# Beginning the first three products of a hybrid SSD / RG-LRU block on half of the tokens

## The chip, the cores and the metric

The kernel runs on one core of one Trainium2 chip. The metric is the device time of one execution in microseconds (us), the median of several executions. A core has a matmul engine (TensorE, PE in the profile, with PEld for its weight loads), a vector engine (VectorE, DVE), a scalar engine (ScalarE, ACT), GpSimd (POOL) and SyncE (SP), which here issues the transfers between main memory and the core's SBUF. Each engine takes its instructions in order, and engines wait for one another on semaphores. PE writes only to PSUM, which has eight banks of 128 partitions by 512 floats.

## The reference

One residual block over x [512 tokens, 1024 channels], float32:

```
h = rmsnorm(x, mix_pre_norm)
u = h @ w_in                                  # [ssd z | ssd x,B,C | ssd dt | lru gate | lru x | merge gates]
y_a = ssd_mixer(u_z, u_xbc, u_dt, ...)        # conv4, chunked state-space scan, gated norm
y_b = rglru_mixer(u_ly, u_lx, ...)            # conv4, gated linear recurrence
merged = g0 * (y_a @ w_proj_ssm) + g1 * (y_b @ w_proj_lru)
x = x + rmsnorm(merged @ w_out, mix_post_norm)
h = rmsnorm(x, ffn_pre_norm)
up = causal_dwconv(h @ w_ffn_up)
x = x + rmsnorm((gelu(up_gate) * up_value) @ w_ffn_down, ffn_post_norm)
```

Here only the first two lines matter: the norm of x along its 1024 channels, and the first three column groups of `h @ w_in`: 128 columns of B (called slab 0), the 16 dt columns padded to a slab (slab 1), and 128 more columns of B (slab 2).

## The kernel before

**Weights.** All weights come as 149 slabs of [128, 1024] floats, in the order of use, loaded one by one on SP's queue into three `raw` buffers. Each slab is split into a high part (`whi`, a cast on ACT) and a low part (`wlo`, a subtraction on DVE), each with three buffers; the dt slab gets no `wlo`, only 16 columns of its `whi` are overwritten with a difference. `prefetch(n)` splits slabs until n of them lie ahead of use, and `low_parts` issues the subtractions that are due.

**Products.** `product(hT)` takes one slab and multiplies it with the activations of all 512 tokens, which are held channel-major in two halves `hT[0]` (high) and `hT[1]` (low), eight tiles of 128 channels each (k = 0 to 7). For each k it issues three matmuls of 128x512 (whi times high, whi times low, wlo times high), 24 for a slab. The dt product issues two for each k, 16 in all.

**The start.** x comes as four token tiles `xts[t]` of [128 tokens, 1024 channels]. For each tile ACT sums the squares (`sumsq`) and takes a root, DVE makes two factors of it by four small instructions (`inv_rms`) and scales the tile (`scale`), and PE turns its eight 128x128 blocks (transposes by a matmul with `ident`) into eight PSUM tiles `tps[k]`, one for each k with all 512 tokens. Ahead of that PE does 24 transposes of `ident` (`WARM`), which use nothing and whose output nobody reads. When all four tiles are turned, the eight `tps[k]` are split into `hT`: `split_scaled` multiplies by the channel's norm weight on ACT (the high part), then takes the difference on DVE (the low part). The splits of slabs 0 and 1 stand among these. Then the products begin.

**What sets the order.** The class `InOrder` keeps ACT's and PE's instructions in the order in which the program writes them, and DVE's until `V.on = False`; after that a scheduler orders DVE. Two engines that read the same PSUM bank wait for each other in the order written. PSUM has eight tiles (`ps`), handed out in turn; a new one waits until the readers of the old one in its bank are done. After each product, `conv` reads its PSUM tile with one ACT and three DVE instructions; `dt_product` copies its result on DVE, and two slabs later `dt_tokens` turns that copy on PE.

The same halving exists before, later in the kernel: around the second norm (`h2_pair`, `early`) the first four products of `w_ffn_up` are begun on tokens 0 to 255, with 128x256 matmuls.

Of the kernel before, what the change touches and what calls it, by code (L numbers as in the profile page):

```python
# [25 lines left out]

# columns of the per-channel parameter array
C_SCW, C_SCB = 0, 48
# [5 lines left out]
N_PC = 356  # L34
# columns of the row parameter array
R_POST, R_POST2, R_HEAD = 0, D, 2 * D
# [3 lines left out]
class InOrder:  # L40
    """An engine whose instructions keep the order in which they are written here."""

# [11 lines left out]
def block_kernel(ctx: ExitStack, tc, x, slabs, wgate, pc, rows, out):  # L54
# [37 lines left out]

# [1 line left out]
    xts = []  # L94
    for t in range(TT):
        xt = quad()
        nc.sync.dma_start(out=xt, in_=x[t * P:(t + 1) * P, :])
        xts.append(xt)
    ident = const.tile([P, P], F32, name="ident")
    make_identity(nc, ident)  # L100
    pcs = const.tile([P, N_PC], F32, name="pcs")
    nc.sync.dma_start(out=pcs, in_=pc)
    hrow = const.tile([P, 48], F32, name="hrow")
    nc.sync.dma_start(out=hrow, in_=rows[0:1, R_HEAD:R_HEAD + 48].partition_broadcast(P))

# [1 line left out]
    pending, steps = [], []  # L107
# [5 lines left out]
    def step(cost, fn, *args):  # L113
        """A step for the vector engine, of that many microseconds."""
        steps.append((cost, fn, args))

    def next_slab():
        """What follows needs the tensor engine to have gone on, or another engine's result."""
        steps.append(None)
# [19 lines left out]

# [1 line left out]
    n_slabs = slabs.shape[0]  # L141
    stream = {"load": 0, "split": 0, "use": 0}
    raws, splits, places, late = {}, {}, {}, []
    AHEAD, EARLY, WARM = 2, 4, 24

# [53 lines left out]
    def split_scaled(hi, lo, src, w):  # L199
        """Split of src * w, w one value per partition."""  # L200
        A.mul(hi, src, w)
        V.scalar_tensor_tensor(out=lo, in0=src, scalar=w, in1=hi.bitcast(F32),
                               op0=ALU.mult, op1=ALU.subtract)
# [7 lines left out]
    def product(acts):  # L211
        """One 128-column slab against [1024, 512] activations: [128 columns, 512 tokens]."""
        w = slab()
        acc = ps()
        accumulate(acc, w, acts)
        return acc

    def conv(acc, w0, bias, taps):
        """Causal depthwise convolution along the tokens."""
        t = tmp()  # L220
        A.activation(t, acc, AF.Identity, bias=pcs[:, bias:bias + 1],
                     scale=pcs[:, w0 + taps - 1:w0 + taps])
# [24 lines left out]

    def inv_rms(parts, width, e):
        """(sum of parts / width + e) ** -0.5, as two factors; one part may be [128, n]."""
        n = parts[0].shape[1]  # L250
# [4 lines left out]
        for s in parts[:-1]:  # L255
# [3 lines left out]
        r = t("root")  # L259
        A.activation(r, parts[-1], AF.Sqrt, scale=1.0 / width, bias=e)  # L260
        v = t("var")
        V.tensor_scalar(out=v, in0=parts[-1], scalar1=1.0 / width, scalar2=e,
                        op0=ALU.mult, op1=ALU.add)
# [12 lines left out]

# [1 line left out]
    use_sqrt()  # L278
    hT = big16("H", F32R), big16("H", F32R)
    junk = work.tile([P, D], F32, tag="M", name="squares", bufs=1)  # L280
    tps = [ps() for _ in range(KT)]
    for k in range(WARM):
        PE.transpose(tps[k % KT][:, 0:P], ident, ident)
    for t in range(TT):
        scale(xts[t], xts[t], inv_rms([sumsq(xts[t], junk=junk)], D, EPS1))
        for k in range(KT):
            transpose(tps[k][:, t * P:(t + 1) * P], xts[t][:, k * P:(k + 1) * P])
    prefetch(1)
    low_parts()
    for k in range(KT):  # L290
        split_scaled(hT[0][:, k, :], hT[1][:, k, :], tps[k], pcs[:, C_PRE + k:C_PRE + k + 1])
        if k == 3:
            prefetch(2)
            low_parts()
    V.on = False

# [1 line left out]
    def causal(value, name):  # L298
        m = const.tile([P, P], F32, name=name)      # value where column >= row
        G.memset(m, value)  # L300
        G.affine_select(out=m, in_=m, compare_op=ALU.is_ge, fill=0.0, base=0,
                        pattern=[[1, P]], channel_multiplier=-1)
        return m
# [4 lines left out]
    G.memset(ones, 1.0)  # L308
    halfb = const.tile([P, 32], F32, name="halfb")  # halves of br, bi, gate_b
    V.tensor_scalar_mul(halfb, pcs[:, C_BR:C_BR + 32], 0.5)  # L310
    nsp4 = const.tile([P, 8], F32, name="nsp4")     # -4 softplus(-lambda)
    nega = const.tile([P, HEADS], F32, name="nega")

    def softplus(u, e):
        """max(u, 0) + log1p(e) with e = exp(-|u|), the logarithm by its atanh series."""
        n = u.shape[1]
# [15 lines left out]

# [1 line left out]
    def ssd_input(j, dst=None):  # L334
# [17 lines left out]
    def dt_product():  # L352
        w = slab()[0]
        acc = ps()
        for k in range(KT):
            c = slice(k * P, (k + 1) * P)
            mm(acc, w[:, c], hT[0][:, k, :], k == 0, False)
            mm(acc, w[:, c], hT[1][:, k, :], False, k == KT - 1)
        raw = tmp()
        V.tensor_copy(raw[:32, :], acc[:32, :])  # L360
        after(2, lambda: dt_tokens(raw))
# [69 lines left out]
    for g in range(2):  # L431
        ssd_input(10 + g, Cc[:, g, :])
        tick()
# [1 line left out]
    xs = big.tile([P, TT, D], F32, tag="C", name="xs", bufs=2)  # L435
# [129 lines left out]

# [1 line left out]
    for j in range(2):  # L567
# [16 lines left out]

# [1 line left out]
    for c in range(2):  # L586
# [80 lines left out]

# [1 line left out]
    m1 = []  # L669
# [23 lines left out]

# [1 line left out]
    def row_tile(r0):  # L695
# [121 lines left out]

# [1 line left out]
    early = []  # L819
# [51 lines left out]
def _layout(x, mix_pre_norm, mix_post_norm, w_in, ssm_conv_w, ssm_conv_b, ssm_dt_bias, ssm_a_log,  # L871
# [70 lines left out]
```

## Time and profile before

| what | value |
|---|---|
| runs | 889.61, 887.66, 887.65 us; median 887.66 |
| the profiled execution | span 885.8 us from first to last instruction; its own time is not listed apart from the three runs |
| what lies around the span, by the median | 887.66 - 885.8 = 1.86 us |
| busy PE / PEld / DVE / ACT / POOL | 872.5 / 724.0 / 519.9 / 392.8 / 1.7 us |
| TensorE clock granted, mean | 0.999 |
| DMA | 91.6 MB, mean 103 GB/s |

The span is what the trace shows of one execution; the time of a run holds some more around it. Busy time of PE counts matmuls from their start to their modelled end. An engine's rows are its instructions in order of time; the note in square brackets is how long it sat idle before the instruction and what ended that.

### The profile page before, as it was taken

Reading aid. Unit: us, or ns where it says so; the run is one execution under the profiler, and the core shown is the slowest. Engines: PE = TensorE matmul, PEld = TensorE weight load, DVE = VectorE, ACT = ScalarE, POOL = GpSimd, SP = SyncE. Lnnn points to the kernel's source line nnn. Section 1 sums busy time; section 2 is a strip of 40 time slices with the busy share of each in tenths; the row PEclk is TensorE's granted clock in tenths of the full one; section 3 lists DMA queues with packets and bytes.
Section 4 is the critical chain, followed back from the end, with each engine's and each line's share of the span. In section 5 each row is a group of like instructions: output and inputs, shape, how many; then the busy total and the mean of one; then the engine's idle time right before and its main releaser. Section 6 shows DMA issues by size and latency. Waiting matters only on the chain.

```text
span 885.8 us, 10176 instructions
## 1 busy us (share of the span) xinstructions
PE 872.5 (98%) x4050; PEld 724.0 (82%) x4050; DVE 519.9 (59%) x732; ACT 392.8 (44%) x602; POOL 1.7 (0%) x14
## 2 busy tenths in 40 slices
PE   7999999999999999999999999999999999999996
PEld 6888887888878888888888988888888888888885
DVE  6777657987874554344467566666666666223225
ACT  6454535579584334222355444444444444213222
POOL 0000000000000000000000000000000000000000
PEclk9999999999999999999999999999999999999999
DMA  6332232222325332222370022222222222322212
GB/s 224 102 137 95 95 118 84 92 87 72 142 96 182 128 119 72 96 95 95 102 252 27 25 94 96 95 95 96 95 95 95 95 95 95 117 98 95 95 48 96
DMA packets 26192, 91.61 MB, mean 103 GB/s; under 512 B 3040, under 2 KB 4256, under 8 KB 25632
## 3 DMA queue, kind: packets, MB, share of 16 engines
q1 hardware_dynamic: 26144, 90.95, 30.1%
q8 instruction: 32, 0.52, 0.2%
q14 instruction: 16, 0.13, 0.0%
HBM read 88.81 MB, written 2.13 MB: 103 GB/s over the span
## 4 chain that ended last, share of the span: by engine, by line
PE 88%; DVE 5%; ACT 5%; issue 1%; DMA 1%; SPq 0%; DVEq 0%; ACTq 0%
PE ps L50 88%; ACT L L50 1%; DVE L L642 1%; DMA raw<-slabs 1%; DVE wlo L180 1%; ACT whi L50 1%; ACT tmp L50 1%; DVE tmp L660 0%; DVE L L636 0%; ACT L50 0%; ACT junk L245 0%; ACT M L50 0%; DVE Y L197 0%; ACT Y L50 0%; ACT junk L50 0%
## 5 line engine op out<-in xcount | busy, mean ns | idle before, releaser
L180 DVE TENSOR_TENSOR wlo<-raw,whi 128x1024 fp32r<-128x1024 f32 x139 | 169.7, 1222 | 140.5 <-ACT whi L50 137.9
L50 PE MATMUL ps<-C,whi 128*128 128x512 f32 x768 | 241.6, 389 | 0.0
L50 PE MATMUL ps<-H,whi 128*128 128x512 f32 x720 | 224.1, 394 | 1.5 <-DVE H L50 1.5
L50 ACT CAST whi<-raw 128x1024 fp32r<-128x1024 f32 x137 | 143.0, 1045 | 110.9 <-PE ps L50 105.6
L50 PEld LDWEIGHTS ps<-C,whi 128*128 128x128 f32 x768 | 144.1, 188 | 29.9
L225 DVE SCALAR_TENSOR_TENSOR tmp<-ps,pcs,tmp 128x511 f32<-128x511 f32 (+1 forms) x156 | 116.6, 748 | 80.4 <-ACT tmp L50 77.9
L50 PE MATMUL ps<-C,wlo 128*128 128x512 f32 x416 | 161.8, 389 | 0.0
L50 PEld LDWEIGHTS ps<-H,whi 128*128 128x128 f32 x720 | 134.1, 188 | 31.1 <-issue 2.4
L50 PE MATMUL ps<-H,wlo 128*128 128x512 f32 x352 | 137.5, 391 | 0.4 <-DVE wlo L180 0.3
L50 ACT ACTIVATE tmp<-ps,pcs 128x512 f32<-128x512 f32 x68 | 53.1, 780 | 128.2 <-PE ps L50 128.2
L50 PEld LDWEIGHTS ps<-C,wlo 128*128 128x128 f32 x416 | 78.1, 188 | 16.1
L50 PE MATMUL ps<-whi,H 128*128 128x512 f32 x256 | 81.4, 394 | 0.0
L50 PEld LDWEIGHTS ps<-H,wlo 128*128 128x128 f32 x352 | 66.1, 188 | 15.2 <-DVE wlo L180 1.2
L50 PE MATMUL ps<-whi,Y 128*128 128x512 f32 x192 | 59.6, 389 | 0.0
L50 PEld LDWEIGHTS ps<-whi,H 128*128 128x128 f32 x256 | 48.1, 188 | 10.3 <-issue 0.5
L50 PE MATMUL ps<-wlo,H 128*128 128x512 f32 x128 | 49.9, 389 | 0.0
L50 ACT CAST Y<-tmp 128x512 fp32r<-128x512 f32 x24 | 14.9, 621 | 66.9 <-DVE tmp L690 36.8
L50 ACT ACTIVATE tmp<-ps,halfb 128x512 f32<-128x512 f32 x32 | 21.5, 687 | 49.6 <-PE ps L50 49.6
L50 PEld LDWEIGHTS ps<-whi,Y 128*128 128x128 f32 x192 | 36.0, 188 | 7.5
L50 PE MATMUL ps<-Y,whi 128*128 128x512 f32 x128 | 40.5, 396 | 0.2 <-DVE Y L197 0.2
L50 PE MATMUL ps<-whi,L 128*128 128x512 f32 x128 | 39.7, 389 | 0.0
L50 PE MATMUL ps<-wlo,Y 128*128 128x512 f32 x96 | 37.3, 389 | 0.0
(167 smaller groups left out, 848.1 us busy)
## 6 DMA issues: line engine op xcount, KB each, us to landing
raw<-slabs SPq DMA_DIRECT2D x149, 512.0 KB, 3.2
quad<-x SPq DMA_DIRECT2D x8, 512.0 KB, 4.3
M<-acsD SPq DMA_DIRECT2D x4, 1024.0 KB, 4.6
out<-tmp SPq DMA_DIRECT2D x8, 256.0 KB, 2.1
wg<-wgate SPq DMA_DIRECT2D x8, 128.0 KB, 3.3
quad<-rows SPq DMA_DIRECT2D x2, 512.0 KB, 4.7
pcs<-pc SPq DMA_DIRECT2D x1, 178.0 KB, 7.1
acsD<-acsT SPq DMA_DIRECT2D x1, 32.0 KB, 2.9
```

The costliest lines, as they stand in the source:

```text
L50: return lambda *args, **kw: self.tc.keep_in_program_order(op(*args, **kw))
L180: V.tensor_sub(*late.pop(0))
L225: V.scalar_tensor_tensor(out=t[:, d:], in0=acc[:, :S - d], scalar=pcs[:, w:w + 1], in1=t[:, d:], op0=ALU.mult, op1=ALU.add)
L642: V.tensor_tensor_scan(out=qq[:, e, :], data0=aa[:, e, :], data1=uu[:, e, :], initial=0.0, op0=ALU.mult, op1=ALU.add)
```

## The change

The four token tiles are handled as two pairs (q = 0: tokens 0 to 255, q = 1: tokens 256 to 511). The eight PSUM tiles `tps` become two groups of four: `tps[q][k // 2]` holds the blocks of two channel tiles for one pair. After tiles 0 and 1 are scaled and turned, the split into `hT` is made for tokens 0 to 255 (`h_hi` on ACT, `h_lo` on DVE, 128x256 each), and among these instructions stand the squares, roots and scalings of tiles 2 and 3. Then PE issues slab 0 on the first half of the tokens, the turning of tile 2, slab 1 on the first half, the turning of tile 3, and slab 2 on the first half; the three PSUM tiles stay open in the list `begun`. Last the split of the second half is issued, by turns on ACT and DVE. `product` and `dt_product` take the first three slabs from `begun` and add the second half. Slab 0 is loaded between token tiles 1 and 2, slabs 1 and 2 after tile 3; `pcs` (the array of per-channel parameters) is loaded on ACT's queue, `hrow` after the slabs; `WARM` is 20. `prefetch` is called behind each of these three products, since three slabs hold all three weight buffers. (Comments and docstrings are removed too.)

```diff
+    def load_x(n):
+        for t in range(len(xts), n):
+            xt = quad()
+            nc.sync.dma_start(out=xt, in_=x[t * P:(t + 1) * P, :])
+            xts.append(xt)
+
+    load_x(2)
+    pcs = const.tile([P, N_PC], F32, name="pcs")
+    nc.scalar.dma_start(out=pcs, in_=pc)
...
-    AHEAD, EARLY, WARM = 2, 4, 24
+    AHEAD, EARLY, WARM = 2, 4, 20
...
     def product(acts):
+        if begun:
+            acc, w = begun.pop(0)
+            accumulate(acc, w, acts, TK[1])
+            prefetch(min(AHEAD, 3 - len(begun)))
+            return acc
...
+    load_slab()
+    load_x(TT)
+    load_slab()
+    load_slab()
+    nc.sync.dma_start(out=hrow, in_=rows[0:1, R_HEAD:R_HEAD + 48].partition_broadcast(P))
...
-    for t in range(TT):
-        scale(xts[t], xts[t], inv_rms([sumsq(xts[t], junk=junk)], D, EPS1))
-        for k in range(KT):
-            transpose(tps[k][:, t * P:(t + 1) * P], xts[t][:, k * P:(k + 1) * P])
-    prefetch(1)
-    low_parts()
-    for k in range(KT):
-        split_scaled(hT[0][:, k, :], hT[1][:, k, :], tps[k], pcs[:, C_PRE + k:C_PRE + k + 1])
-        if k == 3:
-            prefetch(2)
-            low_parts()
+    for t in range(2):
+        norm_root(t)
+    for t in range(2):
+        norm_scale(t)
+        norm_turn(t)
+    split_slab()
+    low_parts()
+    for k in range(KT):
+        h_hi(0, k)
+        if k in (1, 4):
+            norm_root(2 + k // 4)
+    for k in range(KT):
+        h_lo(0, k)
+        if k in (2, 6):
+            norm_scale(2 + k // 6)
+    w = first_weights()
+    begun = [(ps(), w)]
+    accumulate(*begun[0], hT, TK[0])
+    norm_turn(2)
+    split_slab()
+    w = first_weights()
+    begun.append((ps(), w))
+    dt_half(w, begun[1][0], 0)
+    norm_turn(3)
+    split_slab()
+    low_parts()
+    w = first_weights()
+    begun.append((ps(), w))
+    accumulate(*begun[2], hT, TK[0])
+    for k in range(KT):
+        h_hi(1, k)
+        h_lo(1, k)
```

`norm_root(t)` is the squares and the root of tile t on ACT, `norm_scale(t)` the four small DVE instructions and the scaling, `norm_turn(t)` the eight transposes on PE. `TK` is the pair of token halves. `dt_half(w, acc, q)` is the 16 matmuls of the dt slab on half q.

The built order on DVE, from the scaling of the last token tiles on. In the names, `quad` is a token tile, `H` is `hT`, `ps` with its number a PSUM tile. Before, from the scaling of tile 3:

```order
L50 TENSOR_SCALAR quad_81<-quad_81,root_192,step_197 128x1024
L50 TENSOR_TENSOR wlo_212<-raw_209,whi_211 128x1024
L50 SCALAR_TENSOR_TENSOR H_99<-ps_101,pcs_88,H_98 128x512
L50 SCALAR_TENSOR_TENSOR H_99<-ps_102,pcs_88,H_98 128x512
L50 SCALAR_TENSOR_TENSOR H_99<-ps_103,pcs_88,H_98 128x512
L50 SCALAR_TENSOR_TENSOR H_99<-ps_104,pcs_88,H_98 128x512
L50 TENSOR_TENSOR whi_229<-raw_214,whi_229 128x8x16
```

In the change, from the scaling of tile 2 (`quad_93`) over that of tile 3 (`quad_95`) to the low part of slab 2:

```order
L50 TENSOR_SCALAR quad_93<-quad_93,root_183,step_201 128x1024
L50 SCALAR_TENSOR_TENSOR H_105<-ps_108,pcs_79,H_104 128x256
L50 SCALAR_TENSOR_TENSOR H_105<-ps_109,pcs_79,H_104 128x256 x2
L50 SCALAR_TENSOR_TENSOR H_105<-ps_110,pcs_79,H_104 128x256
L50 TENSOR_SCALAR var_209<-ssq_188,eps_87 128x1
L50 RECIPROCAL root_190<-root_190 128x1
L50 SCALAR_TENSOR_TENSOR step_212<-root_190,var_209 128x1
L50 TENSOR_SCALAR step_212<-step_212 128x1
L50 TENSOR_SCALAR quad_95<-quad_95,root_190,step_212 128x1024
L50 SCALAR_TENSOR_TENSOR H_105<-ps_110,pcs_79,H_104 128x256
L50 TENSOR_TENSOR whi_250<-raw_97,whi_250 128x8x16
L50 TENSOR_TENSOR wlo_281<-raw_99,whi_280 128x1024
```

The low part of the last channel tile of the first half (the second row with `ps_110`) now stands behind all five instructions that scale tile 3; before, no low part stood ahead of or between the scalings.

The built order on PE at the start. Before:

```order
L50 MATMUL ps<-ident 128x128 x24
L50 MATMUL ps<-ident,quad 128x128 x32
L50 MATMUL ps<-H,whi 128x512 x2
L50 MATMUL ps<-H,wlo 128x512
L50 MATMUL ps<-H,whi 128x512 x2
```

In the change, from the end of slab 0's first half (the 20 transposes of `ident`, 16 of tiles 0 and 1 and 21 matmuls stand ahead):

```order
L50 MATMUL ps<-H,whi 128x256 x2
L50 MATMUL ps<-H,wlo 128x256
L50 MATMUL ps<-ident,quad 128x128 x8
L50 MATMUL ps<-H,whi 128x256 x16
L50 MATMUL ps<-ident,quad 128x128 x8
L50 MATMUL ps<-H,whi 128x256 x2
L50 MATMUL ps<-H,wlo 128x256
```

The 16 transposes of tiles 2 and 3 now stand behind the first half of slab 0, eight on each side of the dt slab's first half; before, all 32 stood ahead of the first product.

## Rows read from the trace of the kernel before

**Rows 1.** Busy time of each engine over the span, from the page.
```profile
PE 872.5 (98%) x4050; PEld 724.0 (82%) x4050; DVE 519.9 (59%) x732; ACT 392.8 (44%) x602; POOL 1.7 (0%) x14
```

**Rows 2.** Chain that ended last, pieces in time: start us, us, what.
```profile
15.22 168.91 PE ps L50 x782
...
184.16 0.69 ACT tmp L50
```

**Rows 3.** One of PE's waits: waited for, us in total, times, longest.
```profile
PE ps L50 <- DVE H L50: 1.5, 1, 1.5
```

**Rows 4.** Timeline of the start: start us, us, engine, instruction [idle before].
```profile
4.44 1.06 ACT L50 ACTIVATE squares<-quad 128x1024 f32<-128x1024 f32 x1 [2.14 <-DMA quad<-x]
...
5.83 1.04 ACT L50 ACTIVATE squares<-quad 128x1024 f32<-128x1024 f32 x1
...
7.32 0.21 DVE L50 TENSOR_SCALAR var<-ssq,eps 128x1 f32<-128x1 f32 x1
...
7.93 1.06 ACT L50 ACTIVATE squares<-quad 128x1024 f32<-128x1024 f32 x1 [0.64 <-DMA quad<-x]
8.08 0.81 DVE L50 TENSOR_SCALAR quad<-quad,root,step 128x1024 f32<-128x1024 f32 x1
...
8.95 1.09 PE L50 MATMUL ps<-ident,quad 128*128 128x128 f32 x8 [0.39 <-DVE quad L50]
...
12.21 1.05 ACT L50 CAST whi<-raw 128x1024 fp32r<-128x1024 f32 x1 [1.43 <-DMA raw<-slabs]
...
13.16 2.42 ACT L50 ACTIVATE H<-ps,pcs 128x512 fp32r<-128x512 f32 x4
13.29 1.23 DVE L50 TENSOR_TENSOR wlo<-raw,whi 128x1024 fp32r<-128x1024 f32 x1 [0.75 <-ACT whi L50]
14.43 2.72 DVE L50 SCALAR_TENSOR_TENSOR H<-ps,pcs,H 128x512 fp32r<-128x512 f32 x4
...
15.22 0.73 PE L50 MATMUL ps<-H,whi 128*128 128x512 f32 x2 [1.54 <-DVE H L50]
```

**Rows 5.** Timeline of the first three products, to the turning of dt.
```profile
20.80 4.24 PE L50 MATMUL ps<-H,whi 128*128 128x512 f32 x18
...
21.81 2.32 DVE L225 SCALAR_TENSOR_TENSOR tmp<-ps,pcs,tmp 128x511 f32<-128x511 f32 x3 [0.70 <-ACT tmp L50]
...
24.62 0.68 DVE L360 COPY tmp<-ps 32x512 f32<-32x512 f32 x1 [0.49 <-PE ps L50]
...
29.96 0.43 PE L50 MATMUL ps<-ident,tmp 32*128 32x32 f32 x4
```

**Rows 6.** Timeline of PE around the second norm, where products are begun on half.
```profile
492.74 1.91 PE L50 MATMUL ps<-ident,tmp 128*128 128x128 f32 x16
494.40 14.64 PE L50 MATMUL ps<-C,L 128*128 128x256 f32 x120
508.88 0.63 PE L50 MATMUL ps<-C,whi 128*128 128x512 f32 x2
```

**Rows 7.** Timeline of ACT and DVE there, splits of 128x256.
```profile
478.90 2.95 ACT L201 ACTIVATE C<-ps,pcs 128x256 fp32r<-128x256 f32 x7 [0.95 <-PE ps L50]
...
482.31 1.26 DVE L202 SCALAR_TENSOR_TENSOR C<-ps,pcs,C 128x256 fp32r<-128x256 f32 x3
...
483.91 0.47 DVE L202 SCALAR_TENSOR_TENSOR C<-ps,pcs,C 128x256 fp32r<-128x256 f32 x1
...
484.41 0.47 ACT L201 ACTIVATE C<-ps,pcs 128x256 fp32r<-128x256 f32 x1 [0.61 <-DVE C L202]
```

**Rows 8.** Windows of the start (us, busy of PE, PEld, DVE, ACT, POOL, PEclk, DMA share, GB/s).
```profile
2.00:4.00 2.00, 2.00 (x11) 2.00 (x10) 0.00 (x0) 0.29 (x2) 0.35 (x2) 1.00 0.93 328
4.00:6.00 2.00, 2.00 (x12) 2.00 (x11) 0.26 (x2) 1.52 (x4) 0.00 (x0) 1.00 0.89 346
```

**Rows 9.** PE's groups to 16 us, shapes apart: count, busy us, mean ns of one, idle.
```profile
L50 PE MATMUL ps<-ident 128*128 128x128 f32 x24 | 5.0, 402 | 1.6 <-POOL ident masks.py:199 1.6
L50 PE MATMUL ps<-ident,quad 128*128 128x128 f32 x32 | 4.4, 280 | 2.7 <-DVE quad L50 2.7
```

More of the change, by code (lines that the diff above doesn't have):

```diff
@@ L94, in block_kernel @@
     xts = []
-    for t in range(TT):
-        xt = quad()
-        nc.sync.dma_start(out=xt, in_=x[t * P:(t + 1) * P, :])
-        xts.append(xt)
+    def load_x(n):
[6 more added lines that the diff above has]
+    nc.scalar.dma_start(out=pcs, in_=pc)
     ident = const.tile([P, P], F32, name="ident")
     make_identity(nc, ident)
-    pcs = const.tile([P, N_PC], F32, name="pcs")
-    nc.sync.dma_start(out=pcs, in_=pc)
     hrow = const.tile([P, 48], F32, name="hrow")
-    nc.sync.dma_start(out=hrow, in_=rows[0:1, R_HEAD:R_HEAD + 48].partition_broadcast(P))
     pending, steps = [], []
@@ L260, in inv_rms, with inv_root, t @@
         A.activation(r, parts[-1], AF.Sqrt, scale=1.0 / width, bias=e)
+        return inv_root(parts[-1], r, width, e)
+    def inv_root(s, r, width, e):
+        n = s.shape[1]
+        def t(name):
+            return tiny.tile([P, n], F32, tag=f"{name}{n}", name=name, bufs=4 if n == 1 else 1)
         v = t("var")
-        V.tensor_scalar(out=v, in0=parts[-1], scalar1=1.0 / width, scalar2=e,
+        V.tensor_scalar(out=v, in0=s, scalar1=1.0 / width, scalar2=e,
                         op0=ALU.mult, op1=ALU.add)
@@ L280, in block_kernel @@
     junk = work.tile([P, D], F32, tag="M", name="squares", bufs=1)
-    tps = [ps() for _ in range(KT)]
+    tps = [[ps() for _ in range(KT // 2)] for _ in range(2)]
     for k in range(WARM):
-        PE.transpose(tps[k % KT][:, 0:P], ident, ident)
-    for t in range(TT):
-        scale(xts[t], xts[t], inv_rms([sumsq(xts[t], junk=junk)], D, EPS1))
-        for k in range(KT):
-            transpose(tps[k][:, t * P:(t + 1) * P], xts[t][:, k * P:(k + 1) * P])
-    prefetch(1)
+        PE.transpose(tps[0][k % 4][:, 0:P], ident, ident)
@@ new lines, in block_kernel, with norm_root, norm_scale, norm_turn @@
+    root = {}
+    def norm_root(t):
+        q = sumsq(xts[t], junk=junk)
+        r = tiny.tile([P, 1], F32, tag="root1", name="root")
+        A.activation(r, q, AF.Sqrt, scale=1.0 / D, bias=EPS1)
+        root[t] = q, r
+    def norm_scale(t):
+        scale(xts[t], xts[t], inv_root(*root[t], D, EPS1))
+    def norm_turn(t):
+        for k in range(KT):
+            o = (2 * (k % 2) + t % 2) * P
+            transpose(tps[t // 2][k // 2][:, o:o + P], xts[t][:, k * P:(k + 1) * P])
+    TK = slice(0, 2 * P), slice(2 * P, S)
@@ new lines, in h_hi, with h_lo, dt_half @@
+    def h_hi(q, k):
+        A.mul(hT[0][:, k, TK[q]], tps[q][k // 2][:, TK[k % 2]], pcs[:, C_PRE + k:C_PRE + k + 1])
+    def h_lo(q, k):
+        V.scalar_tensor_tensor(out=hT[1][:, k, TK[q]], in0=tps[q][k // 2][:, TK[k % 2]],
+                               scalar=pcs[:, C_PRE + k:C_PRE + k + 1],
+                               in1=hT[0][:, k, TK[q]].bitcast(F32), op0=ALU.mult, op1=ALU.subtract)
+    def dt_half(w, acc, q):
+        for k in range(KT):
+            c = slice(k * P, (k + 1) * P)
+            mm(acc[:, TK[q]], w[0][:, c], hT[0][:, k, TK[q]], k == 0, False)
+            mm(acc[:, TK[q]], w[0][:, c], hT[1][:, k, TK[q]], False, k == KT - 1)
@@ L289, in block_kernel, with first_weights @@
+    def first_weights():
+        i = stream["use"]
+        stream["use"] += 1
+        return splits.pop(i)
+    for t in range(2):
[4 more added lines that the diff above has]
+    split_slab()
     low_parts()
     for k in range(KT):
-        split_scaled(hT[0][:, k, :], hT[1][:, k, :], tps[k], pcs[:, C_PRE + k:C_PRE + k + 1])
-        if k == 3:
-            prefetch(2)
-            low_parts()
+        h_hi(0, k)
+        if k in (1, 4):
+            norm_root(2 + k // 4)
@@ L352, in dt_product @@
     def dt_product():
-        w = slab()[0]
-        acc = ps()
-        for k in range(KT):
-            c = slice(k * P, (k + 1) * P)
-            mm(acc, w[:, c], hT[0][:, k, :], k == 0, False)
-            mm(acc, w[:, c], hT[1][:, k, :], False, k == KT - 1)
+        acc, w = begun.pop(0)
+        dt_half(w, acc, 1)
+        prefetch(min(AHEAD, 3 - len(begun)))
         raw = tmp()
```

## The prediction, made before the changed kernel was run

> **What bounds the kernel now.** The busy times come first [rows 1]: PE is busy for 872.5 of 885.8 us, so only 13.3 us are left to win or to lose by its waiting. The chain of waits says where they lie [rows 2]: from 15.22 us on it runs through PE alone for 168.91 us (782 matmuls), and the ACT work that follows at 184.16 was released by PE. So whatever moves PE's first dense stretch moves all that comes behind it by the same amount; no transfer and no other engine sets a date of its own there. PE's waits [rows 3] show what ended last ahead of 15.22: 1.5 us of waiting for the low part of h on DVE. The question is therefore one of 30 us: when are the first three products done? The marker I use is the turning of dt on PE, the first instruction behind them, at 29.96 [rows 5].
>
> **Prices.** A 512-column matmul comes every (4.24 - 0.39) / 17 = 0.2265 us [rows 5], taking 0.39 as the last one's own length. A 256-column one comes every (508.88 - 494.40) / 120 = 0.1207 us, not half of it, and a transpose every (494.40 - 492.74) / 16 = 0.104 us [rows 6]. A 256-column split costs ACT 2.95 / 7 = 0.42 and DVE 1.26 / 3 = 0.42, each with its result after 0.47 + 0.03 us [rows 7]. Squares and root of one tile hold ACT for 5.83 - 4.44 = 1.39 us. On DVE the four small instructions take 8.08 - 7.32 = 0.76 and the scaling about 0.73 behind them, 1.49 us for a tile; a slab's low part takes 14.43 - 13.29 = 1.14 and a cast 13.16 - 12.21 = 0.95 [rows 4].
>
> **Transfers.** Token tile 0 was there at 4.44 and its squares began then [rows 4]. In the change `pcs` (178 KB) is issued on ACT's queue beside tile 0. The engines already moved 328 to 346 GB/s in these windows at 0.89 to 0.93 of their time [rows 8], so at 0.337 MB/us its 0.182 MB are worth 0.54 us: tile 0 is late by between 0 (another queue costs nothing) and 0.54 us. I take the middle, 0.27, and keep both ends. The Trainium skill (DMA: Bandwidth & Descriptors, section "Issuing engines are not separate DMA queues") says that transfers issued by different engines run on the same 16 DMA engines and interleave, which speaks against this edit: by that rule the full 0.54 is paid, and the sum below would be 0.27 higher. The busy share in the rows fits that rule; no row here shows two queues at once. The edit of the other loads I cost at nothing: slab 0 is third in line, and the third transfer before was in use at 7.93 [rows 4]; with up to 0.54 on top its cast ends at about 9.45. The tiles and slabs behind it are needed later than that by more than a transfer each.
>
> **The path of the first half.** The turning of tile 1 began at 8.95 [rows 4], now at 9.2.
> - ACT: `h_hi` of k = 0 and 1 from about 9.7 (two transposes and their latency, an estimate from their 280 ns [rows 9]), to 10.5; squares and root of tile 2 to 11.9; k = 2 to 4 to 13.2; tile 3 to 14.6; k = 5 to 7 to 15.8; two casts to 17.7.
> - DVE: low part of slab 0 from 9.45 to 10.6, `h_lo` 0 and 1 to 11.45; then it waits for ACT until 12.4; `h_lo` 2 to 12.8; tile 2 to 14.3; four `h_lo` to 16.0; tile 3 to 17.5; the last `h_lo` lands at 18.0.
> - PE: three matmuls for each k as they come, the last two behind that `h_lo`, done at about 18.2.
>
> So slab 0's half is through at 18.2. That is 24 x 0.1207 = 2.90 us of work; without waits it would have begun at 15.3. Beside the 15.22 of before, nothing is won, though PE touches its first product at 11.5: DVE is the engine that sets this stretch, with 1.14 + 8 x 0.42 + 2 x 1.49 = 7.5 us of work from 9.4 on and a wait of 0.95 for ACT.
>
> **What then lies on PE's path.**
> - The turning of tiles 2 and 3 stood in PE's idle time and now stands between dense work: 16 x 0.104 = +1.66 us.
> - 128 matmuls of 256 columns for 64 of 512: 128 x 0.1207 - 64 x 0.2265 = 15.45 - 14.50 = +0.95.
> - The splits of the second half start when two transposes of tile 3 are out, at 18.2 + 0.83 + 1.93 + 0.45 = 21.4. Here ACT's odd k waits for DVE's even k in the same bank, the wait that row 484.41 shows (ACT idle until a `C` of DVE ended at 484.38) [rows 7]. Two k take 0.42 + 0.50 + 0.50 = 1.42, the last low part lands at 21.4 + 0.5 + 0.5 + 3 x 1.42 + 1.0 = 27.7. PE comes to it at 24.7 + 22 x 0.1207 = 27.35: +0.3.
> - dt: slab 3 finds no free weight buffer until slab 0's second half is done at about 28.0; cast (1.05) and low part (1.14) go to 30.2, the convolution of product 0 takes DVE 2.32 [rows 5], to 32.5, and the copy of dt 0.68 behind it, to 33.2. Before, the copy ran at 24.62, five us ahead of need. PE is through with slab 2 at 32.8: +0.4.
> - The 20 instead of 24 warm-up transposes, and `hrow`, cost nothing: nobody reads the first, and `hrow` is first wanted at 30 us.
>
> Sum: 0.1 + 1.66 + 0.95 + 0.3 + 0.4, less the 0.1 that PE also idled before its marker of 29.96, is +3.3 us: the marker at 33.2. The ends are +3.0 and +3.6 by the transfer, and I allow 0.5 more on either side for latencies that I set. Against the profiled execution the span goes from 885.8 to 889.1; with the 1.86 us around it that is 890.9 us, 3.2 above the median of 887.66. Behind the marker the convolutions on DVE run some 2 us later against PE than before; PE has slab 4 split about 2 us ahead of need and DVE has 40% of its time free [rows 1], so I cost that at nothing.
>
> **Rivals.**
> 1. *The clock falls behind the sparse start.* The 24 warm-up transposes took 402 ns on average where the 32 later ones took 280, and they came every (5.0 - 0.4) / 23 = 0.20 us [rows 9] against 0.104 [rows 6]: PE began at the lower of its two levels (1.2 and 2.4 GHz) and left it during the warm-up. That warm-up is now 0.8 us shorter, and between 10.3 and 18.2 PE has 2.9 us of work. For it: one of the three runs was 1.95 us longer. Against it: 32 transposes in 8.6 us held the level before. If the dense work meets the lower level for at most the 5.0 us that the warm-up lasted, it loses at most half, 2.5 us: 893.4. The Trainium skill (TensorE: Matmul & The Clock Gate, section "What's actually happening") says that "the default state is throttled, and activity releases the throttle"; the slow warm-up agrees.
> 2. *The small costs fold away, and the result can't be told from no change.* If DVE does not wait for ACT at 11.45, the bank waits of the second half are hidden and the copy of dt is placed ahead of the convolution, 0.95 + 0.3 + 0.4 fall out of the sum: +1.6, 889.3.
> 3. *Not slower: the early products pay as written.* The mechanism is PE's idle time from 11.5 to 15.22: if `h_lo` 7 landed in time for PE to run slab 0's half without a gap from 11.5, that half would be done at 14.4, 3.8 us earlier, and the sum would be 3.3 - 3.8 = -0.5: 887.1. It decides by the landing of the last `h_lo`: ahead of 14.9 the change is not slower, and DVE's 7.5 us from 9.4 on allow 16.9 at the earliest. Only if rows 4 and 7 overstate DVE here can it hold.
>
> **How the numbers follow.** A measurement of this kernel can tell about 0.3%, 2.7 us, from no change, so the line to "slower" is at 890.3. My forecast has 0.58 and mostly lies above that line (890.2 to 891.6), rival 1 has 0.20 (892 to 893.5), rival 2 has 0.13, rival 3 has 0.06, and 0.03 is for faster by more than 0.3%, for which I have no mechanism. Slower by over 0.3%: nearly all of the forecast and rival 1, 0.74; the same: 0.23; faster: 0.03. The range leaves out rival 3 and the tail of rival 1 and takes in most of rival 2: 889.2 to 893.4.
>
> **What would show it.** Right: PE's first 256-column matmul at about 11.5, and gaps in slab 0's half that wait for DVE's `H`; the last of it near 18; eight transposes on each side of the dt half with no idle time; ACT waits for DVE's `H` in the second half; an idle stretch of PE ahead of the turning of dt, at about 33. The late part should be the same, shifted. Wrong: slab 0's half done by 15, or the marker at 30 or earlier; 256-column matmuls that come slower than every 0.13 us behind 18 would be rival 1; a marker at 33 with an end that has not moved would say that the chain at 184 us is not tied to PE as I read it.

## The result, and the profile after

The changed kernel took 895.4 us (median of five runs, 893.35 to 896.64) beside 889.08 us for the kernel before in the same batch: a ratio of 1.0075 with a 95% interval of 1.0063 to 1.0087, that is 6.3 us more. In a second batch it was 894.35 beside 887.71 (1.0066, 1.0052 to 1.0079). The direction was the one forecast. The size was not: 3.2 us were forecast, and 895.4 lies above the range. (The forecast counted from a median of 887.66 us; with the five runs of this batch the kernel before has 889.08.) The kernel before itself varied between 886.99 and 889.79 over all batches, so each comparison below is with the runs of its own batch.

The page of the profiled execution, which was the shortest of the five (893.35 us):

```profile
span 891.6 us, 10316 instructions
...
PE 876.2 (98%) x4110; PEld 729.6 (82%) x4110; DVE 520.9 (58%) x740; ACT 393.6 (44%) x610; POOL 1.7 (0%) x14
```

Beside [rows 1], PE has 60 more matmuls (64 more in the products, four fewer in the warm-up) and waits 15.4 us instead of 13.3. The span grew by 5.8 us, of which only 2.1 are waiting that the profile calls idle. The rest is PE at work on more, or on slower, instructions.

The timeline of the changed kernel's start (start us, us, engine, instruction, idle time before it), to be read against [rows 4, 5]:

```profile
5.50 1.06 ACT L50 ACTIVATE squares<-quad 128x1024 f32<-128x1024 f32 x1 [2.77 <-DMA quad<-x]
...
8.52 3.45 PE L50 MATMUL ps<-ident,quad 128*128 128x128 f32 x16 [2.63 <-DVE quad L50]
...
10.73 0.84 ACT L50 ACTIVATE H<-ps,pcs 128x256 fp32r<-128x256 f32 x2 [1.45 <-PE ps L50]
...
11.62 0.97 PE L50 MATMUL ps<-H,whi 128*128 128x256 f32 x2
...
16.11 0.58 PE L50 MATMUL ps<-H,whi 128*128 128x256 f32 x1 [1.26 <-DVE H L50]
...
18.62 0.48 DVE L50 SCALAR_TENSOR_TENSOR H<-ps,pcs,H 128x256 fp32r<-128x256 f32 x1
...
19.50 1.03 PE L50 MATMUL ps<-ident,quad 128*128 128x128 f32 x8
20.29 2.16 PE L50 MATMUL ps<-H,whi 128*128 128x256 f32 x16
22.29 1.04 PE L50 MATMUL ps<-ident,quad 128*128 128x128 f32 x8
...
23.74 0.84 ACT L50 ACTIVATE H<-ps,pcs 128x256 fp32r<-128x256 f32 x2 [0.55 <-DVE H L50]
...
28.55 0.88 PE L50 MATMUL ps<-H,whi 128*128 128x256 f32 x2
...
33.92 0.67 DVE L437 COPY tmp<-ps 32x512 f32<-32x512 f32 x1
...
34.64 0.43 PE L50 MATMUL ps<-ident,tmp 32*128 32x32 f32 x4 [0.32 <-DVE tmp L437]
...
59.40 0.66 PE L50 MATMUL ps<-ident,tmp 128*128 128x128 f32 x4 [0.62 <-DVE tmp L419]
```

The marker, the turning of dt on PE, moved from 29.96 [rows 5] to 34.64: +4.7 us in the first 35 us of the kernel. PE does touch its first product at 11.62 instead of 15.22, but waits in it for DVE (1.26 us ahead of 16.11), the last low part lands only at 19.1 (18.62 + 0.48), and the turnings of tiles 2 and 3 follow on PE at 19.50 and 22.29. Two rows were not foreseen: tile 0's squares begin at 5.50 instead of 4.44, and the 16 transposes of tiles 0 and 1 take 3.45 us in one piece, where before eight took 1.09.

The windows of the changed kernel (columns as in [rows 8]) say why those transposes were slow:

```profile
8.00:10.00 2.00, 1.48 (x8) 1.26 (x8) 1.89 (x7) 1.25 (x3) 0.00 (x0) 0.72 1.02 416
10.00:12.00 2.00, 2.00 (x10) 1.89 (x9) 1.48 (x2) 1.27 (x3) 0.00 (x0) 0.50 0.92 358
12.00:14.00 2.00, 1.44 (x7) 0.90 (x6) 0.78 (x3) 1.97 (x7) 0.00 (x0) 0.92 0.74 260
14.00:16.00 2.00, 0.62 (x3) 0.41 (x3) 1.89 (x8) 1.97 (x6) 0.00 (x0) 0.93 0.04 16
16.00:18.00 2.00, 1.89 (x9) 1.90 (x10) 1.89 (x9) 2.00 (x4) 0.00 (x0) 0.50 0.00 0
18.00:20.00 2.00, 1.88 (x12) 1.58 (x12) 2.00 (x4) 0.36 (x1) 0.00 (x0) 0.72 0.00 0
20.00:22.00 2.00, 2.00 (x19) 2.00 (x18) 0.43 (x1) 0.00 (x0) 0.00 (x0) 1.00 0.80 272
```

The column behind POOL is the granted clock. It is 0.50, the lower of PE's two levels (1.2 GHz), in the window from 10 to 12 us and again from 16 to 18; PE had nothing to do from 6 to 8.5 us, and 0.62 us of work from 14 to 16. From 20 us on it stays at 1.00.

What comes after is the old program, later. The scalar engine's read of the same product, of the kernel before and then of the change, at half of the way and near the end:

```profile
433.28 0.69 ACT L50 ACTIVATE tmp<-ps,halfb 128x512 f32<-128x512 f32 x1 [2.42 <-PE ps L50]
...
748.47 0.78 ACT L50 ACTIVATE tmp<-ps,pcs 128x512 f32<-128x512 f32 x1 [3.73 <-PE ps L50]
```

```profile
438.64 0.69 ACT L50 ACTIVATE tmp<-ps,halfb 128x512 f32<-128x512 f32 x1 [2.42 <-PE ps L50]
...
754.12 0.78 ACT L50 ACTIVATE tmp<-ps,pcs 128x512 f32<-128x512 f32 x1 [3.73 <-PE ps L50]
```

It is 5.36 us late at 433 us and 5.65 at 748, with the same idle time before it to the hundredth. So all but 1 us of this loss was there at the marker, 0.6 came in at 59.4 (the last row of the timeline), and nothing was given back.

### The profile page after: what moved, and what is told of

It is laid out like the page before. It is cut to its first block, busy times and chain, and to the rows that moved or that the text cites. A ratio compares the mean times of both kernels' runs of the same rounds, so it can differ in the third digit from the quotient of the medians.

```text
span 891.6 us, 10316 instructions
## 1 busy us (share of the span) xinstructions
PE 876.2 (98%) x4110; PEld 729.6 (82%) x4110; DVE 520.9 (58%) x740; ACT 393.6 (44%) x610; POOL 1.7 (0%) x14
## 4 chain that ended last, share of the span: by engine, by line
PE 84%; DVE 7%; ACT 5%; DMA 2%; issue 1%; DVEq 0%; SPq 0%; ACTq 0%
PE ps L50 84%; DVE wlo L183 1%; DMA wg<-wgate 1%; ACT L L50 1%; DVE L L719 1%; ACT whi L50 1%; ACT tmp L50 1%; DVE H L50 1%; DMA quad<-x 1%; DVE tmp L737 0%; ACT H L50 0%; DVE L L713 0%; ACT junk L253 0%; DVE tmp L233 0%; ACT M L50 0%
## 5 line engine op out<-in xcount | busy, mean ns | idle before, releaser
L50 PE MATMUL ps<-H,whi 128*128 128x512 f32 (+1 forms) x768 | 229.2, 383 | 2.3 <-DVE H L50 1.8
L50 PEld LDWEIGHTS ps<-H,whi 128*128 128x128 f32 x768 | 140.5, 190 | 31.1 <-DVE H L50 3.2
L50 PE MATMUL ps<-H,wlo 128*128 128x512 f32 (+1 forms) x368 | 140.8, 383 | 0.4 <-DVE wlo L183 0.4
L50 PEld LDWEIGHTS ps<-H,wlo 128*128 128x128 f32 x368 | 69.7, 189 | 14.6 <-DVE wlo L183 1.2
```

Source lines behind the costliest of these rows:

```text
L50: return lambda *args, **kw: self.tc.keep_in_program_order(op(*args, **kw))
```

## Experiments

### The clock

`e1_fill` puts transposes of the identity, whose output nobody reads, into PE's idle time:

```diff
-    AHEAD, EARLY, WARM = 2, 4, 20
+    AHEAD, EARLY, WARM = 2, 4, 44
...
-    accumulate(*begun[0], hT, TK[0])
+    def fill(n):
+        for _ in range(n):
+            PE.transpose(tps[1][3][:, 0:P], ident, ident)
+
+    fill(8)
+    for k in range(KT):
+        c = slice(k * P, (k + 1) * P)
+        mm3(begun[0][0][:, TK[0]], w[0][:, c], w[1][:, c], hT[0][:, k, TK[0]], hT[1][:, k, TK[0]],
+            k == 0, k == KT - 1)
+        fill((8, 8, 8, 0, 0, 0, 10, 0)[k])
```

> The changed kernel with transposes of the identity that nobody reads put into PE's idle time: 44 instead of 20 ahead of tile 0, 8 ahead of the first product, 8 each behind k = 0, 1, 2 of slab 0's first half and 10 behind k = 6. Theory (the lower clock level, met because PE is sparse until 19 us, is a part of the loss): the granted clock reads 1.00 in every window from 8 us on, slab 0's half is done 0.5 us earlier than in the profile of the change (19.0 instead of 19.5), and the median falls by 1 to 3 us, since four of the five runs of the change were 1.3 to 3.3 us longer than the profiled one. Rival (ACT and DVE pace this stretch whatever PE's clock is, and the length of the runs has another cause): the clock rises to 1.00 but the median stays within 0.5 us of the change's 895.4.

Measured: 893.43 us beside 888.10 (1.0055, 1.0040 to 1.0070), 5.3 us above the kernel before, where the unaltered change was 6.3 and 6.6 above. Its runs lie within 1 us of each other (892.90 to 893.84). The granted clock reads 1.00 in every window from 6 to 22 us, and the turning of tile 2 begins at 19.01. Half of that lead of 0.49 is tile 0, which came at 5.26 in this execution. So the lower level costs about 1 us in the median of the times; by the spans of the same executions it is more, 1.8 us (4.8 above the kernel before here, 6.6 in the second batch of the change). The granted clock, as a mean over a whole execution, is 0.999 in all four of `e1_fill` and 0.992 to 0.995 in all nine of the change, so the spread of the change goes with it. The rival falls. PE did more work here and the kernel was faster for it.

`e4_warm20` is the kernel before with the change's shorter warm-up and nothing else:

```diff
-    AHEAD, EARLY, WARM = 2, 4, 24
+    AHEAD, EARLY, WARM = 2, 4, 20
```

> The kernel before with 20 instead of 24 transposes of warm-up, nothing else. Theory (the shorter warm-up is a cause of its own, since PE left the lower clock level only at about 6 us, after 20 of them would have ended): the granted clock is below 1.00 in some window between 7 and 20 us, and the median is 1 to 2 us above the kernel before. Rival (20 are enough; it is the sparse first half that loses the level): clock 1.00 and the time within 0.5 us of the kernel before.

Measured: 888.67 beside 888.10 (1.0009, 0.9999 to 1.0018). The clock did fall, in the same place as the first low stretch of the change; the windows of this kernel:

```profile
8.00:10.00 2.00, 1.61 (x11) 1.37 (x10) 1.82 (x8) 1.94 (x6) 0.00 (x0) 0.72 0.30 104
10.00:12.00 2.00, 2.00 (x12) 2.00 (x11) 1.89 (x8) 0.54 (x2) 0.00 (x0) 0.50 1.03 424
12.00:14.00 2.00, 1.47 (x12) 1.24 (x10) 1.45 (x3) 1.95 (x4) 0.00 (x0) 0.93 0.71 291
```

So the shorter warm-up, which I had costed at nothing, can lose the level by itself. That four transposes decide it is not shown: in this batch the mean granted clock of the kernel before was 0.999 in six of 13 executions and 0.997 in seven, whose spans were 1.6 us longer (medians 885.8 and 887.4), and with 20 it was 0.995 to 0.997 in eight of ten. The kernel before thus meets a lower clock in about half of its executions too; that 32 transposes held the level was true of the one that was profiled. The price of the shorter warm-up is small here, 0.6 us with an interval that reaches zero: below the theory's 1 to 2 us, and just above the 0.5 that the rival allowed.

`e9_warm44` is the changed kernel with 44 transposes of warm-up and no other filler.

```diff
-    AHEAD, EARLY, WARM = 2, 4, 20
+    AHEAD, EARLY, WARM = 2, 4, 44
```

> The changed kernel with 44 instead of 20 transposes of warm-up and no other filler, to tell the two low stretches of the clock apart. Theory (the first low stretch, from about 9 us, comes from the warm-up that ends at 5.9, 2.6 us ahead of tile 0; the second, from about 15 us, from the sparse first half of slab 0): the clock reads 1.00 from 8 to 14 us and still falls to 0.5 somewhere between 13 and 22 us; the time lies between the change's 894.4 and the 893.4 of e1_fill. Rival (one cause: with the level held past tile 0 it stays): clock 1.00 throughout, time as e1_fill.

Measured: 893.78 beside 888.09 (1.0069, 1.0052 to 1.0086), 5.7 us above. Its windows:

```profile
12.00:14.00 2.00, 1.28 (x6) 0.88 (x6) 0.78 (x3) 1.97 (x7) 0.00 (x0) 1.00 0.80 258
14.00:16.00 2.00, 0.62 (x3) 0.42 (x3) 1.89 (x8) 1.97 (x6) 0.00 (x0) 1.00 0.10 39
16.00:18.00 2.00, 1.89 (x10) 1.89 (x11) 1.89 (x9) 2.00 (x4) 0.00 (x0) 0.67 0.00 0
18.00:20.00 2.00, 1.53 (x8) 1.23 (x7) 2.00 (x4) 0.36 (x1) 0.00 (x0) 0.50 0.00 0
```

The first low stretch is gone and the second is there: two causes, as the theory had it, as far as one profile of each kernel can show. With the short warm-up the level goes about when tile 0 is turned (from 8.3 to 8.9 us on), and with PE's thin work while slab 0's half waits for DVE (0.62 us from 14 to 16) it goes again, just ahead of the dense stretch.

### Tile 0 and the parameters

`e2_pcs` loads the parameters on SP's queue behind slab 0, and puts the two small readers behind the last split:

```diff
-    pcs = const.tile([P, N_PC], F32, name="pcs")
-    nc.scalar.dma_start(out=pcs, in_=pc)
...
     load_slab()
+    pcs = const.tile([P, N_PC], F32, name="pcs")
+    nc.sync.dma_start(out=pcs, in_=pc)
     load_x(TT)
...
         h_lo(1, k)
+    halfb = const.tile([P, 32], F32, name="halfb")
+    V.tensor_scalar_mul(halfb, pcs[:, C_BR:C_BR + 32], 0.5)
+    lam = const.tile([P, 8], F32, name="lam")
+    V.tensor_scalar_mul(lam, pcs[:, C_LAM:C_LAM + 8], -1.0)
     V.on = False
...
-        V.tensor_scalar_mul(udt[:, NH:], pcs[:, C_LAM:C_LAM + 8], -1.0)
+        V.tensor_copy(udt[:, NH:], lam)
```

> The changed kernel with the per-channel parameters loaded on SP's queue behind slab 0 instead of on ACT's queue beside tile 0 (and the two small DVE instructions that read them put behind the last split, so that they hold up nothing). Theory (the 178 KB beside tile 0 made it 1.06 us late, and everything hangs on tile 0): the first squares begin at 4.4 instead of 5.50, the turning of dt comes 1.0 to 1.1 us earlier than 34.6, the median falls by about 1 us. Rival (tile 0 is late for another cause, or tiles 2 and 3 and slab 1 behind the parameters become late instead): the squares begin at 5.5 still, or the dt marker does not move by more than 0.3 us.

Measured: 893.10 beside 888.10 (1.0051, 1.0036 to 1.0067), 5.0 us above. In its profile tile 0's squares begin at 4.82, but the dt marker stands at 35.10, later than the change's. The timeline of PE in this kernel shows why:

```profile
7.83 3.68 PE L50 MATMUL ps<-ident,quad 128*128 128x128 f32 x16 [1.68 <-DVE quad L50]
...
19.29 1.70 PE L50 MATMUL ps<-ident,quad 128*128 128x128 f32 x8
...
35.10 0.43 PE L50 MATMUL ps<-ident,tmp 32*128 32x32 f32 x4 [0.31 <-DVE tmp L439]
```

Eight transposes at 19.29 take 1.70 us where [rows 4] have 1.09: in this execution PE was still at the lower level at the start of the dense stretch. So the marker did not come earlier, as the theory had said: tile 0 gave 0.68 us, and the lower level took 1.14 more than in the change's first profile (the table at the end of the experiments). The median is 1.3 to 1.6 us nearer to the kernel before than the change's. One profile can't settle the size of this term, but all of them together can. With the parameters beside it, tile 0's squares began at 5.50, 5.26, 5.36 and 5.75 (the change twice, `e1_fill`, `e9_warm44`), in the mean 5.47. In the nine other profiles of this study they began between 4.22 and 4.82, in the mean 4.52. The two groups do not overlap. The edit costs tile 0 0.95 us, where I had bounded it at 0.54. Whether it is the short rows, the second queue or the two together that make it dearer than its bytes was not tried.

`e3_both` has both edits, the fillers and the parameters behind slab 0.

> Both edits, fillers and the parameters behind slab 0. Theory (what the forecast left out was the size of these two terms; its other terms, 1.66 for the turning behind slab 0's half, 0.95 for half-width matmuls, 0.3 and 0.4 for waits, were right): slab 0's half is done at 18.0 to 18.2, the turning of dt comes at 32.9 to 33.4, and the time is 3 to 4 us above the kernel before, not 6.3. Rival (the two edits were not what the forecast missed): still 5 us or more above the kernel before.

Measured: 892.22 beside 888.10 (1.0042, 1.0027 to 1.0057), 4.1 us above, and its runs lie within 1 us (891.81 to 892.78). Its timeline:

```profile
4.51 1.06 ACT L50 ACTIVATE squares<-quad 128x1024 f32<-128x1024 f32 x1 [2.22 <-DMA quad<-x]
...
17.51 0.48 DVE L50 SCALAR_TENSOR_TENSOR H<-ps,pcs,H 128x256 fp32r<-128x256 f32 x1
...
18.39 1.04 PE L50 MATMUL ps<-ident,quad 128*128 128x128 f32 x8
...
21.18 1.03 PE L50 MATMUL ps<-ident,quad 128*128 128x128 f32 x8
...
33.52 0.43 PE L50 MATMUL ps<-ident,tmp 32*128 32x32 f32 x4 [0.30 <-DVE tmp L449]
```

With the two mis-sized terms out, the path is the forecast one, somewhat late. The forecast holds 0.27 for the transfer that is not there now; without it, the last low part was to land at 17.7 (here 18.0), slab 0's half to be done at 17.9 (18.4) and the marker to come at 32.9 (33.52). About 0.2 of this is the longer warm-up, which pushed the turning of tile 1 from 8.95 to 9.18. The time is just above the 3 to 4 us expected; 0.67 of it lies behind the marker (`e11_tokens`, below). The rival, 5 us or more, falls.

### The terms of the sum

`e5_t2` takes `e3_both` and turns tile 2 behind k = 2 of slab 0's half, in PE's idle time:

```diff
-        fill((8, 8, 8, 0, 0, 0, 10, 0)[k])
+        if k == 2:
+            norm_turn(2)
+        else:
+            fill((8, 8, 0, 0, 0, 0, 10, 0)[k])
...
-    norm_turn(2)
     split_slab()
```

The ten fillers behind k = 6 now overwrite one of tile 2's eight turned blocks, so a part of h is left out of the computation; the instructions and their times are not touched by that.

> e3_both with the turning of tile 2 placed behind k = 2 of slab 0's first half, in the time in which PE waits for the next low part, instead of behind that half. Theory (the turning of tiles 2 and 3 is on PE's path because it stands behind slab 0's half; eight transposes cost 0.83 to 0.9 us there): the turning of dt comes 0.8 to 0.9 us earlier than the 33.52 of e3_both, and the end moves as much. Rival (the second half's splits or the copy of dt take the place of the transposes, so that nothing is won): the dt marker moves by less than 0.3 us.

Measured: 891.46 beside 887.71 (1.0035, 1.0023 to 1.0047), 3.8 us above. The marker stands at 33.30, only 0.22 ahead of `e3_both`, which by itself would be the rival. But in this execution the 44 warm-up transposes ran longer, to 9.1 us instead of 8.5, and pushed all that follows. Counted from the last low part of the first half, the marker comes 33.30 - 18.15 = 15.15 us later, in `e3_both` 33.52 - 17.51 = 16.01. So the eight transposes cost 0.86 us where the change has them (0.83 in the sum), and by that count the rival falls. The whole time, 0.3 us nearer to the kernel before than that of `e3_both`, is too close to show it.

`e6_halves` is the kernel before, with the fourth to sixth product in two half-width passes:

```diff
-        accumulate(acc, w, acts)
+        if 4 <= stream["use"] <= 6:
+            accumulate(acc, w, acts, slice(0, 2 * P))
+            accumulate(acc, w, acts, slice(2 * P, S))
+        else:
+            accumulate(acc, w, acts)
```

> The kernel before, with the fourth to sixth product done in two passes of 128x256 matmuls instead of one of 128x512, nothing else: 144 half matmuls for 72 whole ones, at a place where no split holds PE up. Theory (a half costs 0.1207, more than half of 0.2265): what follows the sixth product comes 144 x 0.1207 - 72 x 0.2265 = 1.07 us later against the dt marker. Rival (PE was waiting beside these products anyway, or halves cost half): under 0.3 us.

Measured from the marker to ACT's read of the sixth product: 53.41 - 29.96 = 23.45 us before, 53.84 - 29.54 = 24.30 here. That is +0.85 for 72 matmuls, so a half comes every (72 x 0.2265 + 0.85) / 144 = 0.119 us, and the change's 64 cost 0.75 where the sum has 0.95. The whole time, 888.21 beside 887.71, can't show so little (0.9990 to 1.0010).

`e11_tokens` takes `e3_both` and lets the first x group be turned a slab later:

```diff
-        after(2, lambda s=s, j=j: to_tokens(s, xs[:, :, j * P:(j + 1) * P]))
+        after(3 if j == 0 else 2, lambda s=s, j=j: to_tokens(s, xs[:, :, j * P:(j + 1) * P]))
```

> e3_both with the turning of the first x group's tokens due one slab later (three instead of two), nothing else. Theory (0.6 us of the loss arise behind the dt marker, since DVE's convolutions run later against PE and PE waits 0.62 us at 58.3 for the tile that it turns): that wait is gone, the lead over the kernel before grows by under 0.1 us between the dt marker and 90 us instead of by 0.67, and the time falls by 0.6. Rival (the same lag makes PE wait at the next place, so nothing is won): PE idles 0.4 us or more elsewhere before 90 us.

Measured: the wait of 0.62 us is gone, and no other takes its place in PE's waits:

```profile
PE ps L50 <- POOL ident masks.py:199: 1.6, 1, 1.6
PE ps L50 <- DVE wlo L181: 0.3, 1, 0.3
PE ps L50 <- DVE tmp L449: 0.3, 1, 0.3
PE ps L50 <- DVE Y L198: 0.2, 1, 0.2
PE ps L50 <- DVE H L50: 0.2, 1, 0.2
```

From the marker (34.47) to ACT's read at 88.94 the distance to the kernel before grows by 0.03 us, where it grew by 0.67 in `e3_both` (33.52 to 88.63; before, 29.96 to 84.40). The time does not show it: 892.08 beside 888.09 (1.0054, 1.0039 to 1.0070). In its profile the warm-up ended late again, so that tile 1 was turned at 10.13 instead of 9.18, which would hide a gain of 0.6 in that execution. The wait is explained; that its removal shortens the kernel is not shown.

### What ended last before

`e7_slab0` has no halving. It is the kernel before with slab 0 loaded right behind the four token tiles, the two small readers behind the splits as in `e2_pcs` (not shown below), and fillers:

```diff
-    pcs = const.tile([P, N_PC], F32, name="pcs")
-    nc.sync.dma_start(out=pcs, in_=pc)
-    hrow = const.tile([P, 48], F32, name="hrow")
-    nc.sync.dma_start(out=hrow, in_=rows[0:1, R_HEAD:R_HEAD + 48].partition_broadcast(P))
...
-    AHEAD, EARLY, WARM = 2, 4, 24
+    AHEAD, EARLY, WARM = 2, 4, 32
...
+    load_slab()
+    pcs = const.tile([P, N_PC], F32, name="pcs")
+    nc.sync.dma_start(out=pcs, in_=pc)
+    load_slab()
+    load_slab()
+    hrow = const.tile([P, 48], F32, name="hrow")
+    nc.sync.dma_start(out=hrow, in_=rows[0:1, R_HEAD:R_HEAD + 48].partition_broadcast(P))
...
             transpose(tps[k][:, t * P:(t + 1) * P], xts[t][:, k * P:(k + 1) * P])
+        for _ in range((3, 6, 4, 0)[t]):
+            PE.transpose(tps[7][:, 3 * P:S], ident, ident)
...
```

> No halving: the kernel before with slab 0 loaded right behind the four token tiles and ahead of the parameters and of the small row (both of short rows), the two small DVE instructions that read the parameters put behind the splits, 32 instead of 24 transposes of warm-up and 3, 6 and 4 of them behind the turning of tiles 0, 1 and 2. Theory (what ended last ahead of 15.22 was the landing of slab 0 at 12.2, then its cast and low part, not the number of tokens): slab 0's cast begins at 10.8, its low part at 12.5 right behind the scaling of tile 3, the first product at 14.3 to 14.5, and the time falls by 0.6 to 1.0 us against the kernel before. Rival (the first low part of h waits for PE's and ACT's share of tile 3 anyway, or tile 3 lands later): first product at 15.2, time the same.

Measured: 886.80 beside 887.71, a ratio of 0.9988 (0.9979 to 0.9997): faster than both kernels. The first product began at 13.59.

`e10_order` is the same without the fillers and with the 24 transposes of before, so that the order of the loads and the place of the two small readers alone differ from the kernel before.

> e7_slab0 without its fillers and with 24 transposes of warm-up: only the order of the loads and the place of two small DVE instructions differ from the kernel before. Theory (e7's gain is the earlier slab 0): the first product begins 0.8 us or more ahead of 15.22 and the time is 0.5 to 1.0 us below the kernel before, as e7_slab0. Rival (the fillers made the gain, by holding the clock): the time is within 0.3 us of the kernel before.

Measured: 886.83 beside 888.09, 0.9985 (0.9976 to 0.9994), 1.3 us faster. Its timeline, against [rows 4]:

```profile
4.51 1.06 ACT L50 ACTIVATE squares<-quad 128x1024 f32<-128x1024 f32 x1 [2.22 <-DMA quad<-x]
...
10.52 1.03 ACT L50 CAST whi<-raw 128x1024 fp32r<-128x1024 f32 x1
...
12.13 1.22 DVE L50 TENSOR_TENSOR wlo<-raw,whi 128x1024 fp32r<-128x1024 f32 x1
12.27 1.09 PE L50 MATMUL ps<-ident,quad 128*128 128x128 f32 x8 [0.39 <-DVE quad L50]
...
13.36 2.73 DVE L50 SCALAR_TENSOR_TENSOR H<-ps,pcs,H 128x512 fp32r<-128x512 f32 x4
```

Slab 0's cast moved from 12.21 to 10.52, its low part from 13.29 to 12.13 and the first low part of h from 14.43 to 13.36. PE's first product began at 14.17 instead of 15.22. What ended last ahead of 15.22 was slab 0 behind the parameters and the small row, and its earlier start can be had without halving anything. But the clock has a part in the 1.3 us: the mean granted clock was 0.998 or more in all ten executions of `e10_order` and in five of the 13 of the kernel before beside it. Against those five the span is 0.5 us shorter (885.1 and 885.6); why the level goes less often with this order of loads was not tried. `e8_change`, the unaltered change in the batch of `e7_slab0`, is the second result quoted at the top.

> The changed kernel once more, unaltered, so that its median stands beside the others' in the same batch. Theory: 5.5 to 7.5 us above the kernel before, its runs spread over 2 us or more; the granted clock falls below 1.00 in some stretch between 8 and 20 us, not at the same place in each execution. Rival: as long as the profiled one in the first batch each time (4.5 to 5.5 above), with the clock low in the same two stretches.

In its profile the clock was low from 8.3 to 11.7 and from 15.1 to 22 us, longer than in the first profile and into the dense stretch, and the dt marker stood at 35.97. Beside `e1_fill` (34.13, with tile 0 0.10 earlier) that prices the lower level at 1.7 us in this execution.

Times from the traces of six kernels with the halving (us) split the way to the marker in two, at the start of the last low part of the first half:

| kernel | squares of tile 0 | last low part | marker | from squares to low part | from low part to marker |
|---|---|---|---|---|---|
| the change, profiled first | 5.50 | 18.62 | 34.64 | 13.12 | 16.02 |
| the change, `e8_change` | 5.36 | 18.70 | 35.97 | 13.34 | 17.27 |
| `e2_pcs` | 4.82 | 18.17 | 35.10 | 13.35 | 16.93 |
| `e9_warm44` | 5.75 | 18.63 | 35.05 | 12.88 | 16.42 |
| `e1_fill` | 5.26 | 18.13 | 34.13 | 12.87 | 16.00 |
| `e3_both` | 4.51 | 17.51 | 33.52 | 13.00 | 16.01 |

In the last two PE was at its upper level all along the second stretch, and it takes them 16.0 us. The lower level cost 1.7 us in `e8_change` and 1.4 in `e2_pcs`, most of it in that stretch, but only 0.3 in the execution of the change that was profiled first, all of it ahead of the last low part.

## Why the prediction was right in its mechanism and wrong in its size

- *PE bounds the kernel from 15.22 on, and a shift of the start moves the end*: right. The same instruction is 5.36 us late at 433 us with the same idle time before it.
- *DVE sets the first half, nothing is won by PE's early start*: right. With the transfer and the clock put aside (`e3_both`) the last low part landed at 17.99; the forecast without the transfer is 17.7.
- *The turnings stand on PE's path (1.66)*: right; eight cost 0.86 (`e5_t2`, counted from the last low part), so 16 about 1.7.
- *Half-width matmuls (0.95)*: right in kind, 0.75 by `e6_halves`.
- *The splits of the second half wait bank by bank (0.3), the copy of dt holds PE up (0.4)*: right in kind. ACT waits 0.55 us for DVE at 23.74, as the row at 484.41 had shown [rows 7]; ahead of the last low part of that half PE loses 0.48 (two matmuls take 0.88 us at 28.55 instead of 0.40), and its wait for the copy is 0.32.
- *The parameters beside tile 0 (0 to 0.54, taken as 0.27)*: this step failed. I priced the transfer by bytes at the rate of the windows [rows 8]. It cost 0.95 us in the mean of 13 profiles, and 1.06 between the two that were compared. The rule of the Trainium skill (DMA: Bandwidth & Descriptors, section "Issuing engines are not separate DMA queues"), that transfers from several issuing engines share the same 16 DMA engines, pointed the right way, and the runs agree with it. The 0.54 that I worked out beside it was still too low.
- *The warm-up costs nothing, and the sparse half loses the clock with a chance of 0.2*: this step failed. In both profiles of the unaltered change PE was at the lower level in two stretches, and either edit of the change is enough for one of them (`e4_warm20`, `e9_warm44`). Its price, 0.3 and 1.7 us in these two profiles and about 1 us in the median (`e1_fill`), was within the 2.5 that the rival allowed. The argument against it, that the level was held before, held for about half of the executions of the kernel before (`e4_warm20`). What was wrong was to give it 0.2 and to set it beside the forecast, when it adds to it.
- *The lag of DVE's convolutions behind the marker (nothing)*: this step failed too. PE waited 0.62 us at 59.4, and `e11_tokens` removed just that wait. I had checked the slabs' low parts against PE's need, not the tiles that PE turns.

The sum as measured, for the execution that was profiled first: 3.25 as forecast (33.2 - 29.96), 0.8 more for tile 0 (1.06 instead of 0.27), 0.25 for the clock (13.12 instead of 12.87 in the table), and 0.3 behind the last low part (16.0 also with the clock held, where the forecast has 33.2 - 17.5 = 15.7) make 4.6 (the marker shows 4.68); 0.62 behind it and 0.3 at the second norm make 5.5 to 5.6, and the row at 754.12 shows 5.65. The 0.3 at the second norm is a wait of PE for a scaled tile that is there in this profile and not in those of `e3_both` or `e5_t2`; why was not tried. The medians lie 6.3 and 6.6 above the kernel before: other executions lost more to the clock, as `e8_change` did.

## What to carry to other kernels

Before beginning a product on half of its rows, see whether the engines that make those rows have time to spare; here DVE had little, so PE's early start became waiting, and the work that had filled the waiting before (the transposes) moved behind it. Read first what ended last ahead of the dense stretch: here it was one slab behind two small transfers, and moving those let the first product start 1.05 us earlier; the kernel was 1.3 us faster, a part of it by the clock. And cost a thinner start of PE at its lower clock as well, as a term of the sum with the price of the rows, not only as an accident.

## What the runs showed of the hardware

- A transfer of 178 KB in rows of 1.4 KB on another engine's queue delayed a 512 KB transfer beside it by 0.95 us, where its bytes at 337 GB/s are worth 0.54.
- PE fell back to its lower level between 8 and 9 us with 20 warm-up transposes that ended at 5.6 to 5.9 (the change twice, `e4_warm20`), and held it with 24 that ended at 6.6 in the profile before. Executions of one kernel differ: the kernel before had a mean granted clock of 0.999 in six and of 0.997 in seven of 13 executions (batch of `e4_warm20`), the change's runs spread over 3.3 us, those of `e1_fill` over 0.9.
- The PEclk column is no proof of the level at the start of a trace. In `e2_pcs` it reads 1.00 in the windows from 8 to 12 us, while 16 transposes took 3.68 us, as slow as the change's 3.45 at 0.50 and 0.72. The durations decide.
- A longer warm-up is not free either: in `e5_t2` and `e11_tokens` the 44 transposes lasted to 9.1 and 9.4 us, where those of `e1_fill` ended at 8.0, and tile 0, scaled at about 7.5, had to wait for PE.
